# Seams between out product and FFN: residual stores and row scaling on GpSimd, more residual buffers, the last tile's squares and transposes placed

## The chip, the cores and the metric

The kernel runs on one core of a Trainium2 chip. The metric is the device time of one execution in microseconds (us); "before" was timed in 3 runs. Engines go by the names of the profile: PE is TensorE, PEld its weight load, DVE VectorE, ACT ScalarE, POOL GpSimd, SP the engine that issues most DMAs.

## The reference, cut to what matters

Two layers on 1024 tokens of width 1024. Layer 0 mixes with two groups of attention heads, layer 1 with a recurrent block. Each layer ends with a SwiGLU feed-forward network (FFN) of width 2816. Every sub-layer has a norm ahead of it and one behind it:

```
def rmsnorm(x, g):
    y = x * lax.rsqrt(jnp.mean(x * x, axis=-1, keepdims=True) + RMS_EPS)
    return y * g

for layer in range(2):
    h = rmsnorm(x, norm_mix_pre[layer])
    m = mixer(h)                       # ends with a product by w_out
    x = x + rmsnorm(m, norm_mix_post[layer])
    h = rmsnorm(x, norm_ffn_pre[layer])
    f = (silu(h @ w_gate) * (h @ w_up)) @ w_down
    x = x + rmsnorm(f, norm_ffn_post[layer])
```

## The kernel before, in words

Nearly every product is made in three passes: each operand is split into a high part (an ACT cast, L96, L525, L620, L736) and a low part (a DVE subtraction, L89, L526, L621, L737), and PE adds high by high, high by low and low by high. The FFN products go by Strassen's scheme: seven block products for gate and up (`strassen` in `gate_up`, L545 to L547 are its matmuls), and a like scheme in `down` (L625 to L627).

The program runs attention, `out_product`, `gate_up`, `down`, the recurrent block, `out_product`, `gate_up`, `down`. The text says seam A for the passage from the first `out_product` to the first `gate_up` (about 590 to 640 us), seam B for the second (about 1580 to 1620 us), and the two `down` stages are down(0) (its end at about 1250 us) and the last down (2140 us to the end).

`out_product` makes the mixer's product in eight tiles of 128 tokens: tiles 0 to 2 and 3 to 5 in three passes, tiles 6 and 7 as plain matmuls (L458). After each tile come two norms. `post_norm` loads the tile's old residual rows (`self.load`, L188, into one of the `nx` buffers), squares the product on ACT (L171; two halves, whose sums POOL adds, L173), makes 1/sqrt on POOL (L174, L175), multiplies by the gain on DVE (L219), adds the residual on DVE (L222) and stores the new residual by SP (L224). `pre_norm` squares that row again (L171), goes through POOL again, scales the row on ACT (L196), and PE turns it (eight transposes of 128x128, L204). `HiddenS.take` copies the turned halves out of PSUM (L85) and builds the right operands of the seven Strassen products, `hS`: high and low parts of the blocks themselves, and of four differences `tf` of them (L89 makes these differences on DVE, then L96 and L89 split them). `down` calls the same two norms for its own eight tiles of 128 rows; down(0) feeds the recurrent block through `HiddenT` (L57, L58), and the last down stores to the output and has no `pre_norm`.

`gate_up` makes the first gate block in two halves of tokens: the early half (tiles 0 to 3) and then the late half (tiles 4 to 7). So the early half's 84 matmuls can run while tiles 4 to 7 are still in their norms. Its weights, `raw`, are first multiplied by the norm's gain (L514, eight ACT instructions of 128x256 for one weight block).

What sets the order: each engine's queue is written by a scheduler of the framework when the kernel is built, from the dependencies, the buffers of each pool (`bufs`) and its own costs; `issue_after(x)` forbids it to place an instruction ahead of x. On the chip each engine takes its queue strictly in order.

Of the kernel before, what the change touches and what calls it, by code (L numbers as in the profile page):

```python
# [61 lines left out]
class HiddenS:  # L62
# [18 lines left out]
    def take(self, t, pst, scratch, pool):  # L81
# [7 lines left out]
        sub = lambda o, x, y: nc.vector.tensor_tensor(o, x, y, op=ALU.subtract)  # L89
        sub(tf[:, 0], b12, b11)  # L90
# [3 lines left out]
        cols = slice(64 * t, 64 * t + 64)  # L94
        for src, (h, l) in zip((hf[:, :, :, lo], hf[:, 1:2, :, hi], tf), self.g):
            self.last = nc.scalar.copy(h[:, :, :, cols], src).ins  # L96
            sub(l[:, :, :, cols], src, h[:, :, :, cols].bitcast(F32))


class Trunk:  # L100
# [64 lines left out]
    def rstd(self, pool, parts, junk):  # L165
# [4 lines left out]
        for p, o in zip(parts, ss):  # L170
            self.squared = nc.scalar.activation(junk, p, AF.Square, accum_out=o).ins  # L171
        if len(parts) == 2:
            nc.gpsimd.tensor_tensor(ss[0], ss[0], ss[1], op=ALU.add)  # L173
        nc.gpsimd.tensor_scalar(rs, ss[0], 1.0 / D, EPS, op0=ALU.mult, op1=ALU.add)  # L174
# [15 lines left out]
    def pre_norm(self, pool, x, h, g, sink, t, psum):  # L190
# [4 lines left out]
        if g is None:  # L195
            nc.scalar.activation(h, x, AF.Copy, scale=rs)  # L196
        else:
            self.scaled = nc.vector.scalar_tensor_tensor(h, x, rs, g, op0=ALU.mult, op1=ALU.mult).ins
        pst = []
        for q in range(2):  # L200
            ps = psum()
            for j in range(4):
                kt = 4 * q + j
                nc.tensor.transpose(ps[:, j * P:(j + 1) * P], h[:, kt * P:(kt + 1) * P], self.ident)  # L204
            pst.append(ps.rearrange("p (a b) -> p a b", a=4))
        sink.take(t, pst, h, pool)

    def post_norm(self, ms, mg, x_src, x_dst, t, gpost, sink, pool):
# [3 lines left out]
        x = pool.tile([P, D], F32, tag="nx", bufs=2, name=self.uid("x"))  # L212
# [5 lines left out]
        for c, m in ms:  # L218
            nc.vector.tensor_tensor(mg[:, c], m, gpost[:, c], op=ALU.mult)  # L219
        if mg is not ms[0][1]:  # L220
            rs = self.rstd(pool, [m for _, m in ms], junk)
        nc.vector.scalar_tensor_tensor(x, mg, rs, x, op0=ALU.mult, op1=ALU.add)  # L222
        for k, (d, s) in enumerate(rows(t, x_dst)):
            (nc.scalar if k and sink is None else nc.sync).dma_start(s, x[d, :])  # L224
        if sink is not None:
            self.pre_norm(pool, x, mg, None, sink, t, self.psum_t)
# [217 lines left out]
    def out_product(self, ap, aT, w, x_src, x_dst, gpost_v, sink, kts):  # L444
# [16 lines left out]
        def norm(t, ps):  # L461
            mg = ap.tile([P, D], F32, tag="mg", bufs=3, name=self.uid("mg"))
            ms = [(slice(i * 512, (i + 1) * 512), p) for i, p in enumerate(ps)]
            self.post_norm(ms, mg, x_src, x_dst, t, gpost, sink, ap)
# [517 lines left out]
```

## Time and profile before

| | |
|---|---|
| runs timed | 2254.22, 2256.64, 2258.45 us; median 2256.64 |
| the profiled execution | 2259.16 us, its span in the trace 2257.4 us |
| PE busy | 2209.1 us, 98% of the span |
| DVE busy | 1550.9 us, 69% |
| ACT busy | 1148.2 us, 51% |
| POOL busy | 166.8 us, 7% |

The profiled execution is 2.5 us above the median, and 1.76 us of it lie outside the span. A line such as L204 is a line of the kernel before, as printed above; the kernel after has other numbers. In a row of the timeline the first number is the start in us from the span's start, the second the duration, and the square brackets hold the idle time just before and what ended it.

### The profile page before, as it was taken

The page shows a single profiled execution, that of the slowest core. Times are in us where ns is not written, and L with a number is a line of the kernel's source. Part 1 is how long each engine was busy: PE and PEld are TensorE (multiplying, and loading weights), DVE is VectorE, ACT ScalarE, POOL GpSimd, SP SyncE. Part 2 cuts the span into 40 slices and gives each one's busy share as a digit, 9 for nine tenths or more (in the row PEclk, how much of TensorE's full clock was granted, in tenths as well). Part 3 has the DMA queues.
Part 4 walks back from the last instruction along what each step waited for, and adds up shares of the span by engine and source line. Part 5 has one row for each costly group of instructions (what it writes and reads, how often), then busy time and mean ns, then how long its engine had stood idle before and what let it go on. Part 6 is the DMA issues. An engine that isn't in the chain of part 4 may idle for free. (4 is left out here: it accounts for less than half of the span.)

```text
span 2257.4 us, 30651 instructions
## 1 busy us (share of the span) xinstructions
PE 2209.1 (98%) x11166; PEld 1810.3 (80%) x11166; DVE 1550.9 (69%) x2517; ACT 1148.2 (51%) x2132; POOL 166.8 (7%) x370
## 2 busy tenths in 40 slices
PE   8999999999999999999999999999999999999997
PEld 8888888877688888888887777887788888888875
DVE  5776765464677777776767787536777767669665
ACT  4545455464765444432436567527755454425433
POOL 2111212131100000000001100001100000000010
PEclk9999999999999999999999999999999999999998
DMA  5101011125623323235558511358233333237476
GB/s 169 45 29 34 24 43 46 54 98 151 222 88 111 119 89 122 89 131 184 173 163 256 135 52 47 90 185 270 76 117 107 112 99 118 93 112 267 130 203 189
DMA packets 187131, 273.12 MB, mean 121 GB/s; under 512 B 13922, under 2 KB 115298, under 8 KB 186979
## 3 DMA queue, kind: packets, MB, share of 16 engines
q1 hardware_dynamic: 186338, 269.06, 37.8%
q10 hardware_dynamic: 640, 2.10, 0.3%
q8 instruction: 88, 1.44, 0.3%
q14 instruction: 65, 0.52, 0.1%
HBM read 205.57 MB, written 65.54 MB: 120 GB/s over the span
## 5 line engine op out<-in xcount | busy, mean ns | idle before, releaser
L545 PE MATMUL ps<-hS,q 128*128 128x512 f32 (+1 forms) x1288 | 491.4, 383 | 2.8 <-ACT hS L96 2.8
L546 PE MATMUL ps<-hS,q 128*128 128x512 f32 (+1 forms) x1288 | 491.3, 382 | 0.0
L547 PE MATMUL ps<-hS,q 128*128 128x512 f32 (+1 forms) x1288 | 489.8, 382 | 0.0
L526 DVE TENSOR_TENSOR q<-raw,q 128x512 fp32r<-128x512 f32 x308 | 204.5, 686 | 176.9 <-ACT q L525 176.4
L545 PEld LDWEIGHTS ps<-hS,q 128*128 128x128 f32 x1288 | 244.1, 190 | 49.6 <-ACT hS L96 3.4
L546 PEld LDWEIGHTS ps<-hS,q 128*128 128x128 f32 x1288 | 244.3, 190 | 46.6 <-DVE hS L89 0.4
L547 PEld LDWEIGHTS ps<-hS,q 128*128 128x128 f32 x1288 | 244.4, 190 | 45.7
L525 ACT CAST q<-raw 128x512 fp32r<-128x512 f32 x308 | 177.4, 616 | 166.2 <-DVE raw L534 136.8
L626 PE MATMUL ps<-o,o 128*128 128x512 f32 x616 | 241.3, 392 | 2.8 <-DVE o L621 2.8
L627 PE MATMUL ps<-o,o 128*128 128x512 f32 x616 | 238.9, 392 | 0.5 <-DVE o L737 0.5
L625 PE MATMUL ps<-o,o 128*128 128x512 f32 x616 | 221.4, 393 | 10.3 <-ACT o L736 6.2
L514 ACT ACTIVATE raw<-raw,gcol 128x256 f32<-128x256 f32 x352 | 150.2, 498 | 149.9 <-DMA raw<-in_ffn_w_up_dram 73.0
L620 ACT CAST o<-raw 128x512 fp32r<-128x512 f32 x206 | 123.7, 620 | 197.6 <-PE ps L627 56.7
L621 DVE TENSOR_TENSOR o<-raw,o 128x512 fp32r<-128x512 f32 x206 | 137.8, 688 | 65.2 <-ACT o L620 64.5
L625 PEld LDWEIGHTS ps<-o,o 128*128 128x128 f32 x616 | 116.1, 189 | 38.4 <-ACT o L620 7.4
L626 PEld LDWEIGHTS ps<-o,o 128*128 128x128 f32 x616 | 116.5, 189 | 28.9 <-DVE o L621 4.7
L151 DVE TENSOR_TENSOR wlo<-raw,whi 128x1024 fp32r<-128x1024 f32 x76 | 92.8, 1222 | 65.7 <-ACT whi L150 63.5
L627 PEld LDWEIGHTS ps<-o,o 128*128 128x128 f32 x616 | 116.4, 189 | 24.8 <-DVE o L737 0.9
L174 POOL TENSOR_SCALAR rs<-ss 128x1 f32<-128x1 f32 x64 | 30.2, 472 | 1275.5 <-ACT junk L171 1171.2
L150 ACT CAST whi<-raw 128x1024 fp32r<-128x1024 f32 x76 | 79.8, 1052 | 59.2 <-PE ps L162 24.7
L365 ACT COPY pt<-tr 128x512 f32<-128x512 f32 (+1 forms) x128 | 65.5, 528 | 81.1 <-PE tr L361 80.5
L161 PE MATMUL psq<-hT,whi 128*128 128x512 f32 x256 | 101.2, 395 | 1.1 <-DVE v L260 1.1
(193 smaller groups left out, 4249.5 us busy)
## 6 DMA issues: line engine op xcount, KB each, us to landing
raw<-in_ffn_w_down_dram SPq DMA_DIRECT2D x96, 256.0 KB, 4.4
raw<-in_ffn_w_gate_dram SPq DMA_DIRECT2D x44, 512.0 KB, 4.3
raw<-in_ffn_w_up_dram SPq DMA_DIRECT2D x44, 512.0 KB, 4.4
gS<-c SPq DMA_DIRECT2D x88, 256.0 KB, 3.7
raw<-gS SPq DMA_DIRECT2D x88, 256.0 KB, 2.9
gA<-c SPq DMA_DIRECT2D x66, 256.0 KB, 3.3
raw<-in_attn_w_in_dram SPq DMA_DIRECT2D x24, 512.0 KB, 4.1
raw<-in_attn_w_out_dram SPq DMA_DIRECT2D x24, 512.0 KB, 4.5
```

The costliest lines, as they stand in the source:

```text
L161: nc.tensor.matmul(ps, wh[:, kt, cols], hh[:, kt, :], start=kt == 0, stop=False)
L514: nc.scalar.activation(raw[:, i], raw[:, i], AF.Copy, scale=gain[:, 4 * k + i:4 * k + i + 1])
L525: self.last = nc.scalar.copy(t[:, 0], src).ins
L526: nc.vector.tensor_tensor(t[:, 1], src, t[:, 0].bitcast(F32), op=ALU.subtract)
L545: nc.tensor.matmul(ps, a[:, 0, kt, :], bh, start=kt == 0, stop=False)
L546: nc.tensor.matmul(ps, a[:, 0, kt, :], bl, start=False, stop=False)
L547: nc.tensor.matmul(ps, a[:, 1, kt, :], bh, start=False, stop=kt == 3)
L620: nc.scalar.copy(t[:, 0], src)
L621: tt(t[:, 1], src, t[:, 0].bitcast(F32), op=ALU.subtract)
L625: nc.tensor.matmul(ps, a[0], b[:, 0], start=first, stop=False)
L626: nc.tensor.matmul(ps, a[0], b[:, 1], start=False, stop=False)
L627: nc.tensor.matmul(ps, a[1], b[:, 0], start=False, stop=last)
```

## The change

- `rstd` has the mean's factor in the square (`scale=D ** -0.5`) and adds EPS to the first half's sum, so after the last square POOL has two instructions where it had three for sums of two parts.
- `pre_norm` without a gain scales the row on GpSimd, as two instructions of 128x512, and the residual is stored from GpSimd's DMA queue, in the code behind the scaling. In the last down the stores of seven tiles go by GpSimd, those of the last tile by SP and ACT.
- The residual buffers `nx` go from two to three (tile 5 of `out_product` uses a further one), and in the last down there are four. To make room, `act` has two buffers instead of three.
- Tiles 6 and 7: both `post_norm` are written first, then both `pre_norm`; tile 6's `take` is issued after tile 7's squares and gain product (`last_m`).
- `gate_up`: the gain products of the first gate and up weights (16 instructions of 128x256 for each layer) move from ACT to GpSimd; the splits S3, S1 and S4 of the first gate block come after `last_m`; the last product of the early half (`A22`, 12 matmuls) comes after tile 7's last transpose (`turned`).
- `HiddenS.take` splits the plain blocks first, then makes the differences `tf` and splits them, and the single block last.

```diff
@@ HiddenS.take
+        def split(src, g):
+            h, l = (o[:, :, :, cols] for o in g)
+            self.last = nc.scalar.copy(h, src).ins
+            sub(l, src, h.bitcast(F32))
+
+        split(hf[:, :, :, lo], self.g[0])
         sub(tf[:, 0], b12, b11)
         sub(tf[:, 2], b22, b12)
         sub(tf[:, 1], b22, tf[:, 0])
         sub(tf[:, 3], tf[:, 1], b21)
-        cols = slice(64 * t, 64 * t + 64)
-        for src, (h, l) in zip((hf[:, :, :, lo], hf[:, 1:2, :, hi], tf), self.g):
-            self.last = nc.scalar.copy(h[:, :, :, cols], src).ins
-            sub(l[:, :, :, cols], src, h[:, :, :, cols].bitcast(F32))
+        split(tf, self.g[2])
+        split(hf[:, 1:2, :, hi], self.g[1])
@@ rstd
-        for p, o in zip(parts, ss):
-            self.squared = nc.scalar.activation(junk, p, AF.Square, accum_out=o).ins
-        if len(parts) == 2:
-            nc.gpsimd.tensor_tensor(ss[0], ss[0], ss[1], op=ALU.add)
-        nc.gpsimd.tensor_scalar(rs, ss[0], 1.0 / D, EPS, op0=ALU.mult, op1=ALU.add)
+        eps = EPS
+        for i, (p, o) in enumerate(zip(parts, ss)):
+            self.squared = nc.scalar.activation(junk, p, AF.Square, scale=D ** -0.5, accum_out=o).ins
+            if i < len(parts) - 1:
+                nc.gpsimd.tensor_scalar(o, o, eps, None, op0=ALU.add)
+                eps = o
+        nc.gpsimd.tensor_scalar(rs, ss[-1], eps, None, op0=ALU.add)
         nc.gpsimd.tensor_tensor(rs, rs, self.neghalf, op=ALU.pow)
@@ pre_norm
         if g is None:
-            nc.scalar.activation(h, x, AF.Copy, scale=rs)
+            for i in range(2):
+                cs = slice(i * 512, (i + 1) * 512)
+                nc.gpsimd.tensor_scalar(h[:, cs], x[:, cs], rs, 1.0, op0=ALU.mult, op1=ALU.mult)
+            then()
...
-        sink.take(t, pst, h, pool)
+        with self.behind(behind):
+            sink.take(t, pst, h, pool)
@@ post_norm
-        x = pool.tile([P, D], F32, tag="nx", bufs=2, name=self.uid("x"))
+        if x is None:
+            x = pool.tile([P, D], F32, tag="nx", bufs=3, name=self.uid("x"))
...
+        self.last_m = [self.squared, scaled]
         nc.vector.scalar_tensor_tensor(x, mg, rs, x, op0=ALU.mult, op1=ALU.add)
-        for k, (d, s) in enumerate(rows(t, x_dst)):
-            (nc.scalar if k and sink is None else nc.sync).dma_start(s, x[d, :])
-        if sink is not None:
-            self.pre_norm(pool, x, mg, None, sink, t, self.psum_t)
+        def store():
+            for k, (d, s) in enumerate(rows(t, x_dst)):
+                (stores or [nc.gpsimd] * 2)[k].dma_start(s, x[d, :])
+        if sink is None:
+            store()
+        if later is not None:
+            later.append(lambda b: self.pre_norm(pool, x, mg, None, sink, t, self.psum_t, b, store))
+        elif sink is not None:
+            self.pre_norm(pool, x, mg, None, sink, t, self.psum_t, then=store)
@@ out_product
+            x = self.apool.tile([P, 1152], F32, tag="first", name=self.uid("x"))[:, :D] if t == 5 else None
+            self.post_norm(ms, mg, x_src, x_dst, t, gpost, sink, ap, later, x)
...
-            norm(6 + t, ps)
+            norm(6 + t, ps, later)
+        for pre, b in zip(later, (self.last_m, ())):
+            pre(b)
@@ gate_up, load
-                        nc.scalar.activation(raw[:, i], raw[:, i], AF.Copy, scale=gain[:, 4 * k + i:4 * k + i + 1])
+                        g = gain[:, 4 * k + i:4 * k + i + 1]
+                        if j == 0:
+                            nc.gpsimd.tensor_scalar(raw[:, i], raw[:, i], g, 1.0, op0=ALU.mult, op1=ALU.mult)
+                        else:
+                            nc.scalar.activation(raw[:, i], raw[:, i], AF.Copy, scale=g)
...
-            split("S3", a21)
-            split("S1", a22)
-            tt(a12, a12, a11, op=ALU.subtract)
-            split("S4", a12)
+            with self.behind(behind):
+                split("S3", a21)
+                split("S1", a22)
+                tt(a12, a12, a11, op=ALU.subtract)
+                split("S4", a12)
@@ gate_up, strassen
-            tt(u3, u3, product(new(), q["A22"], 6, cols), op=ALU.subtract)
+            with self.behind(behind):
+                p4 = product(new(), q["A22"], 6, cols)
+            tt(u3, u3, p4, op=ALU.subtract)
@@ gate_up
-            qg = load(wg, j, ["w"] * 7, self.last if j == 1 else None)
+            qg = load(wg, j, ["w"] * 7, self.last if j == 1 else None, () if j else self.last_m)
...
-                strassen([first[:, i] for i in range(4)], qg, early)
+                strassen([first[:, i] for i in range(4)], qg, early, [self.turned])
@@ down
-            with make_sink() as sink:
+            with make_sink() as sink, self.pool("late", "right") as late:
+                if sink is not None:
+                    late = None
...
+                    stores = [nc.sync, nc.scalar] if sink is None and (r, a) == (0, 3) else None
+                    x = late.tile([P, D], F32, tag="nx", bufs=4, name=self.uid("x")) if late else None
+                    self.post_norm(ms, mg, x_src, x_dst, (r, a), gpost, sink, ap, None, x, stores)
```

Three places show what this does to the order. The first is seam A, where PE passes from the early half of the first gate block to the late half; `ps_6761` (before) and `ps_6767` (after) hold the early half's last product, `mg_6522` and `mg_6496` tile 7's scaled row, `ps_6779` the late half's first product. PE before:

```order
L545 MATMUL ps_6761<-hS_5640,q_6656 128x256
L546 MATMUL ps_6761<-hS_5641,q_6656 128x256
L547 MATMUL ps_6761<-hS_5640,q_6656 128x256
L204 MATMUL pst_6544<-ident,mg_6522 128x128 x4
L204 MATMUL pst_6549<-ident,mg_6522 128x128 x4
L545 MATMUL ps_6779<-hS_5636,q_6650 128x256
```

PE after, at the same place, where twelve matmuls on `ps_6767` in all follow the transposes before the late half starts:

```order
L597 MATMUL ps_6753<-hS_5638,q_6661 128x256
L224 MATMUL pst_6550<-ident,mg_6496 128x128 x4
L224 MATMUL pst_6555<-ident,mg_6496 128x128 x4
L595 MATMUL ps_6767<-hS_5640,q_6662 128x256
L596 MATMUL ps_6767<-hS_5641,q_6662 128x256
L597 MATMUL ps_6767<-hS_5640,q_6662 128x256
```

Tile 7's transposes have moved ahead of the early half's last product. DVE at the same place, before, where `mg_6459` is tile 6's row, `tf_6493` and `tf_6556` are the differences of tiles 6 and 7, and `hS_5641` is the low part of the differences:

```order
L89 TENSOR_TENSOR hS_5641<-tf_6398,hS_5640 128x16x64
L571 TENSOR_TENSOR first_6675<-first_6675,ps_6761 128x256
L89 TENSOR_TENSOR tf_6493<-mg_6459 128x256 x2
L89 TENSOR_TENSOR tf_6493<-mg_6459,tf_6493 128x256
L89 TENSOR_TENSOR tf_6493<-tf_6493,mg_6459 128x256
L89 TENSOR_TENSOR hS_5637<-mg_6522,hS_5636 128x8x64
L89 TENSOR_TENSOR hS_5639<-mg_6522,hS_5638 128x4x64
L89 TENSOR_TENSOR hS_5641<-tf_6493,hS_5640 128x16x64
L89 TENSOR_TENSOR tf_6556<-mg_6522 128x256 x2
```

DVE after (`mg_6463` and `tf_6531` are tile 6's, `mg_6496` and `tf_6562` tile 7's):

```order
L89 TENSOR_TENSOR tf_6531<-mg_6463 128x256 x2
L624 TENSOR_TENSOR first_6681<-first_6681,ps_6767 128x256
L89 TENSOR_TENSOR hS_5637<-mg_6496,hS_5636 128x8x64
L89 TENSOR_TENSOR hS_5639<-mg_6496,hS_5638 128x4x64
L89 TENSOR_TENSOR tf_6531<-mg_6463,tf_6531 128x256
L89 TENSOR_TENSOR tf_6531<-tf_6531,mg_6463 128x256
L89 TENSOR_TENSOR hS_5641<-tf_6531,hS_5640 128x16x64
L575 TENSOR_TENSOR q_6904<-raw_6892,q_6904 128x512
L89 TENSOR_TENSOR tf_6562<-mg_6496 128x256 x2
```

The second half of tile 6's differences now stands behind tile 7's plain blocks. The second place is POOL in seam A for tiles 6 and 7. Before:

```order
L173 TENSOR_TENSOR ss_6466<-ss_6466,ss_6467 128x1
L174 TENSOR_SCALAR rs_6465<-ss_6466 128x1
L175 TENSOR_TENSOR rs_6465<-rs_6465,neghalf 128x1
L174 TENSOR_SCALAR rs_6475<-ss_6476 128x1
L175 TENSOR_TENSOR rs_6475<-rs_6475,neghalf 128x1
L173 TENSOR_TENSOR ss_6529<-ss_6529,ss_6530 128x1
L174 TENSOR_SCALAR rs_6528<-ss_6529 128x1
L175 TENSOR_TENSOR rs_6528<-rs_6528,neghalf 128x1
```

POOL after (`x_6464` and `x_6497` are the residual rows of tiles 6 and 7):

```order
L252 DMA xs_89<-x_6464 128x1024
L181 TENSOR_SCALAR ss_6503<-ss_6503 128x1
L183 TENSOR_SCALAR rs_6502<-ss_6504,ss_6503 128x1
L184 TENSOR_TENSOR rs_6502<-rs_6502,neghalf 128x1
L183 TENSOR_SCALAR rs_6511<-ss_6512 128x1
L184 TENSOR_TENSOR rs_6511<-rs_6511,neghalf 128x1
L215 TENSOR_SCALAR mg_6463<-x_6464,rs_6511 128x512 x2
L252 DMA xs_89<-x_6497 128x1024
L183 TENSOR_SCALAR rs_6542<-ss_6543 128x1
L184 TENSOR_TENSOR rs_6542<-rs_6542,neghalf 128x1
L215 TENSOR_SCALAR mg_6496<-x_6497,rs_6542 128x512 x2
L561 TENSOR_SCALAR raw_6898<-raw_6898,gcol 128x256 x4
```

Stores and scaling have entered the queue; the store of tile 7's residual stands ahead of tile 7's second 1/sqrt. The third place is SP in the last down, where the weights and left operands of the product `p3` are loaded (`raw`) and residual rows (`x`) move. Before:

```order
L718 DMA raw_19412<-in_ffn_w_down_dram 128x512
L224 DMA out_dram<-x_19230 64x1024
L188 DMA x_19256<-xs_91 64x1024
L224 DMA out_dram<-x_19243 64x1024
L188 DMA x_19256<-xs_91 64x1024
L717 DMA raw_19433<-gS_1_7_14574 128x512
```

SP after:

```order
L776 DMA raw_19439<-in_ffn_w_down_dram 128x512
L197 DMA x_19649<-xs_91 64x1024
L775 DMA raw_19460<-gS_1_7_14598 128x512
L776 DMA raw_19460<-in_ffn_w_down_dram 128x512
L775 DMA raw_19481<-gS_1_8_14599 128x512
L776 DMA raw_19481<-in_ffn_w_down_dram 128x512
```

The stores have left SP's queue, and of the loads one half row is left ahead of the `raw` with number 7: `x_19649` belongs to the fifth tile and takes a buffer that the first tile's store has to leave.

More of the change, by code (lines that the diff above doesn't have):

```diff
@@ L489, in out_product @@
             rows.append(raw)
-            acts.append(act(kt, 6, 2, ap, 3, ("act", "ah", "al")[i % 3]))
+            acts.append(act(kt, 6, 2, ap, (3, 3, 2)[i % 3], ("ah", "al", "act")[i % 3]))
+        later = []
         for t in range(2):
```

35 lines of the change are left out of this document (23 added, 12 removed).

## Prediction, made before the changed kernel had run

> **What bounds the kernel now.** I read the page first (busy shares and the granted clock), then PE's waits by line and longest case, then the timeline of each place where a long wait stands.
>
> ```profile
> PE 2209.1 (98%) x11166; PEld 1810.3 (80%) x11166; DVE 1550.9 (69%) x2517; ACT 1148.2 (51%) x2132; POOL 166.8 (7%) x370
> ```
>
> ```profile
> PE ps L625 <- ACT o L736: 6.2, 3, 3.5
> PE pst L204 <- ACT mg L196: 5.7, 2, 2.9
> PE ps L625 <- ACT o L620: 4.0, 4, 1.7
> ...
> PE ps L626 <- DVE o L621: 2.8, 4, 2.1
> PE ps L545 <- ACT hS L96: 2.8, 2, 1.4
> ```
>
> PE is the bound nearly everywhere; it has 48.3 us of idle time in all (2257.4 less 2209.1). The columns of the second fence are us in total, cases and the longest. Two of its lines belong to the seams: 5.7 us for the scaled row before tile 7's transposes and 2.8 us for the high parts behind them, two cases each, so about 4.25 us for each seam. The other three belong to the two `down` stages. But a wait costs more than its own length, as a table of stretches of seam A shows (columns: stretch, its length, busy PE, PEld, DVE, ACT, POOL, granted clock, DMA share, GB/s):
>
> ```profile
> 600.00:612.00 12.00, 12.00 (x35) 5.77 (x34) 9.61 (x16) 8.33 (x15) 1.78 (x4) 1.00 0.16 51
> 612.00:627.00 15.00, 12.76 (x102) 11.94 (x100) 14.79 (x31) 13.30 (x28) 3.52 (x7) 0.99 0.42 137
> 627.00:631.00 4.00, 1.99 (x9) 1.59 (x9) 2.70 (x7) 2.50 (x5) 0.00 (x0) 0.50 0.01 2
> 631.00:637.00 6.00, 6.00 (x27) 5.78 (x27) 4.59 (x8) 3.12 (x6) 0.00 (x0) 0.50 0.00 0
> ```
>
> From 612 to 627 DVE is full and ACT nearly; then PE starves, and the granted clock is 0.50 until 637. Two matmuls of 256 columns stand 0.12 us apart at full clock and 0.21 us apart at 0.50:
>
> ```profile
> 624.36 0.28 PE L546 MATMUL ps<-hS,q 128*128 128x256 f32 x1
> 624.48 0.28 PE L547 MATMUL ps<-hS,q 128*128 128x256 f32 x1
> 627.69 1.97 PE L204 MATMUL pst<-ident,mg 128*128 128x128 f32 x8 [2.93 <-ACT mg L196]
> 630.98 0.80 PE L545 MATMUL ps<-hS,q 128*128 128x256 f32 x2 [1.32 <-ACT hS L96]
> ...
> 632.30 0.41 PE L545 MATMUL ps<-hS,q 128*128 128x256 f32 x1
> 632.52 0.41 PE L546 MATMUL ps<-hS,q 128*128 128x256 f32 x1
> ...
> 636.57 0.85 PE L545 MATMUL ps<-hS,q 128*128 128x256 f32 x4
> ```
>
> So each us at half clock loses 0.44 us of matmul work (1 less 0.12/0.213). The Trainium skill ("TensorE: Matmul & The Clock Gate", part 1) describes a gate that looks at PE's activity in windows of a few us; the 0.50 of these rows agrees with its half clock, and nothing below is taken from it.
>
> **Seam A, term by term.** Tile 7's last plain matmul ends at about 612.7, yet its way to the transposes is long:
>
> ```profile
> 618.43 0.60 ACT L171 ACTIVATE junk<-ps 128x512 bf16<-128x512 f32 x1
> ...
> 620.59 0.22 ACT L171 ACTIVATION_READ_ACCUMULATOR junk<-ps 128x1 f32 x1
> ...
> 624.20 1.06 ACT L171 ACTIVATE mg<-x 128x1024 f32<-128x1024 f32 x1 [1.47 <-DVE x L222]
> ...
> 626.49 1.15 ACT L196 ACTIVATE mg<-x,rs 128x1024 f32<-128x1024 f32 x1 [0.20 <-POOL rs L175]
> ...
> 635.07 1.05 ACT L96 CAST hS<-tf 128x1024 fp32r<-128x1024 f32 x1 [2.88 <-DVE tf L89]
> ```
>
> The first square waits 5.7 us in ACT's queue, behind tile 6's scaling, casts and copies. From their end (620.81) to the transposes (627.69) it takes 6.9 us. In the new order they stand ahead of tile 6's second square, so they can end at 615.5: 612.7, two squares of 0.8, and 1.2 us for ACT work in front. Behind them the chain is the same but for POOL's part:
>
> ```profile
> L343 POOL TENSOR_SCALAR pr<-pr,sm 128x512 f32<-128x512 f32 x8 | 5.5, 695 | 7.1 <-DVE sm L342 7.1
> L343 POOL TENSOR_SCALAR pr<-pr,sm 128x256 f32<-128x256 f32 x8 | 3.8, 482 | 6.5 <-DVE sm L342 5.3 <-PE sc L329 0.9
> ```
>
> A scaling of 128x512 by a column takes 0.70 us on POOL (attention has the same instruction), so a row costs 1.39 us where ACT took 1.15: 0.24 more. One POOL instruction less saves 0.28. The store now in front of the second 1/sqrt is issued by POOL, which no row of before shows; the nearest is SP's issue, 0.34 us, and the far end I set at 1.45 us, the longest a POOL instruction took beside a busy DVE:
>
> ```profile
> 624.20 0.34 SPq L224 DMA_DIRECT2D xs<-x  x1
> ```
>
> ```profile
> 2178.68 0.19 POOL L174 TENSOR_SCALAR rs<-ss 128x1 f32<-128x1 f32 x1 [571.38 <-ACT junk L171]
> 2178.95 1.45 POOL L175 TENSOR_TENSOR rs<-rs,neghalf 128x1 f32<-128x1 f32 x1
> ```
>
> I take 0.34 for the store since POOL writes no tile for it, and add 1.0 us because tile 6's 1/sqrt and scaling stand in POOL's queue ahead of tile 7's second part. Transposes ready: 615.5 + 6.9 + 0.24 - 0.28 + 0.34 + 1.0 = 623.7, against 627.69; ends of the unknown costs 622.7 and 626. PE arrives there at 624.6 less the twelve matmuls moved behind (12 x 0.12 = 1.44), so 623.2: a wait of 0.5 us instead of 2.93. At full clock eight transposes take 1.0 us, so they end at 624.7 instead of 629.66.
>
> What is late next are the differences `tf`, made and split on DVE:
>
> ```profile
> 613.88 0.69 DVE L526 TENSOR_TENSOR q<-raw,q 128x512 fp32r<-128x512 f32 x1
> 614.48 0.42 DVE L89 TENSOR_TENSOR tf<-tf,mg 128x256 f32<-128x256 f32 x1
> ```
>
>  Before, the high part was ready at 636.12, 6.5 us after the transposes, and the late half's third product began at 636.57; the slow clock hid that wait. In the new order, between tile 7's transposes and its `tf`, DVE also has two differences of tile 6 (0.42 each) and a split of the up weights (0.69); 1.5 us more, 8.0 in all, so 632.7. PE covers from 624.7 only the twelve moved matmuls (1.44), a short wait of about 0.6 for the plain blocks, and 24 matmuls of the late half (2.88): until 629.6. There a new wait of 3.1 us appears, ended by ACT's cast of `tf`. The third product begins at 632.7 instead of 636.57: 3.9 us won; bounds 1.5 (transposes at 626) and 5.4 (no extra DVE work in the way). A wait like this one brought a half clock of 3.4 us or more in some cases (2.93 us here did) and none in another (2.11 us at 2187.65, below), so I charge half of 3.4 x 0.44 = 1.5 us. Seam A: 3.9 - 0.75 = about 3.1 us won.
>
> **The cover of what moves off ACT and SP.** The 16 gain products of a layer (0.48 us each on POOL) cost PE nothing as long as POOL is through with the early ones before tile 3; POOL works 1.78 of 12 us there before. The stores leave SP, where nothing waited for them in seam A. Three residual buffers end this idle time of DVE, which was not PE's:
>
> ```profile
> 596.65 1.28 DVE L222 SCALAR_TENSOR_TENSOR x<-mg,rs,x 128x1024 f32<-128x1024 f32 x1 [5.51 <-DMA x<-in_x_dram]
> ```
>
> Its worth is that DVE enters the full stretch with less in arrears; without it I would not trust the 1.2 us above.
>
> **Seam B** has the same order:
>
> ```profile
> 1615.14 1.04 ACT L96 CAST hS<-tf 128x1024 fp32r<-128x1024 f32 x1 [2.88 <-DVE tf L89]
> ```
>
> ```profile
> 1608.53 1.09 PE L204 MATMUL pst<-ident,mg 128*128 128x128 f32 x8 [2.77 <-ACT mg L196]
> ```
>
> PE comes to the transposes at 1608.53 - 2.77 - 1.44 = 1604.3 and by the same 0.5 us of wait and 1.0 of work ends them at 1605.8; plus 8.0 is 1613.8 against 1616.2 for the cast's end before: 2.4 won, less 0.75: 1.6 us.
>
> **The down stages.** In the last down these are the long waits of PE, and SP's queue around the first:
>
> ```profile
> 2187.65 0.50 PE L626 MATMUL ps<-o,o 128*128 128x512 f32 x1 [2.11 <-DVE o L621]
> 2196.93 1.19 PE L625 MATMUL ps<-o,o 128*128 128x512 f32 x4 [1.69 <-ACT o L620]
> ...
> 2217.48 0.79 PE L625 MATMUL ps<-o,o 128*128 128x512 f32 x1 [3.51 <-ACT o L736]
> ```
>
> ```profile
> 2184.09 0.51 SPq L224 DMA_DIRECT2D out_dram<-x  x1
> 2187.91 0.45 SPq L188 DMA_DIRECT2D x<-xs  x1
> ...
> 2189.77 0.72 SPq L717 DMA_DIRECT2D raw<-gS  x1
> ```
>
> The wait of 1.69 us is for the `raw` issued at 2189.77, which stood behind a residual load that waited 3.3 us for a store to land. Four buffers take three of four such loads away. The fifth tile's half load still stands ahead of that same `raw`, now behind a store from POOL's queue, so I count that wait as it is (bounds 1.7 won, 1.5 lost). The wait of 2.11 us is DVE's: in the new order more of the norms' work stands ahead of that split, up to two of DVE's 1.28 us steps, so 0 to 1.5 lost; the smaller waits behind may win 1. Sum zero, -3 to +3. The 3.51 us wait is for a load in a stretch that the DMA engines fill; it stays. In down(0) a wait of 2.01 us (cast L736, at 1247.5) ends with a load whose buffer DVE frees; no store stands in front, so I count 0.5 won from ACT's and SP's lighter queues, -2 to +1.5. At the end of the program POOL's chain loses one instruction:
>
> ```profile
> 2249.90 0.19 POOL L173 TENSOR_TENSOR ss<-ss,ss 128x1 f32<-128x1 f32 x1 [3.56 <-ACT junk L171]
> 2250.18 0.19 POOL L174 TENSOR_SCALAR rs<-ss 128x1 f32<-128x1 f32 x1
> ```
>
> That is 0.28 us, all of it on the path.
>
> Sum: 3.1 + 1.6 + 0.5 + 0 + 0.3 = 5.5 us won, so 2253.7 for the profiled execution's 2259.16. That execution stands 2.5 above the median; against the median of 2256.64 the forecast is 2251.
>
> **The rivals.**
>
> Slower: POOL and DVE shut each other out in the seams. The pair at 2178.68 and 2178.95 speaks for it: 0.19 us alone, 1.45 where 0.55 is usual, while DVE ran. POOL's six instructions on tile 7's way (two for 1/sqrt twice, two for the scaling) would each take 0.9 us more (1.45 less 0.55), 5.4 in all: transposes ready at 629.1 instead of 627.69, ended at 630.1, the third product at 638.1 by the same 8.0, 1.5 us later than before; with 1.2 for the half clock that goes on behind it, 2.7 lost at each seam. With one us lost in the last down: 2256.64 + 2 x 2.7 + 1 = 2263. DVE, busy for 31.7 of the 37 us from 600 to 637, has little room to wait for POOL in turn. It turns to a loss once the mean stretch passes about 0.65 us, where its six times eat the 3.9 won. Against it: in the seam before, L174 and L175 ran at 0.38 and 0.55 us beside tile 7. The Trainium skill ("SBUF — State Buffer", section "SBUF: two separate sides") says that a DVE instruction with two SBUF inputs and a GpSimd instruction reading SBUF hold one port pair as an exclusive lock, so that the later one waits for the whole of the other. By that rule the shut-out would be complete and the seams would win nothing; DVE's instructions at the seam mostly have two SBUF inputs, but the short stretches of the row at hand do not bear a full shut-out out. It also says ("DMA: Bandwidth & Descriptors", section "SWDGE vs HWDGE vs iDMA") that GpSimd writes a DMA's descriptors itself, which SP's and ACT's queues don't need; no row of before shows a price.
>
> Full recovery: the new wait for `tf` is short, the half clock does not come, and the stores' leaving SP ends the 1.69 us. Each seam then wins its 4.25 us of waits and the 0.44 of its half clock, 4.25 + 0.44 x 6 = 6.9 us in seam A (10 us at half clock less the 4 idle in it), I take 5.5 for B, where the half clock is shorter, and the down stages 2: about 2242. Against it: DVE's list behind the transposes has not become shorter.
>
> Nothing to measure: the transposes come early, but the late half stands as long for `tf`, and the half clock comes with that wait. Each seam wins 1 us or less: 2255.
>
> **How the numbers follow.** Forecast (1.5 to 9 us won) 0.42; full recovery 0.15; nothing to measure 0.20; slower 0.23. The range leaves out the outer half of the second and the last: 2242 to 2262. The forecast's own range is 2247.5 to 2255. About 0.2%, 4.5 us, can be told from no change. Three quarters of the forecast's chance and all of the full recovery lie under 2252.1: 0.47 faster; the rest of the forecast, the third rival and a little of the slower case make 0.31; slower 0.22.
>
> **What would show it.** Right: in seam A tile 7's squares before 616, its transposes before 625, a new wait of PE ahead of the late half's third product ended by the cast of `tf`, and a granted clock of 0.50 for under 7 us. Wrong: POOL scalings well over 0.70 us each with DVE busy beside them; PE waits at tile 6's transposes, which now stand behind tile 7's squares; PE waits in the last down that grow by more than 2 us because the `raw` with number 7 comes late.

## The result, and the profile after

The changed kernel takes 2294.64 us (median of 4 runs, 2291.13 to 2294.91), the kernel before 2256.03 in the runs beside it: 1.68% slower, ratio 1.0168 with a 95% interval of 1.0156 to 1.018. The forecast was 2251, the range ended at 2262. The span of the profiled execution is 2292.8 us. First the page's busy shares, then PE's waits by line (total us, cases, longest), of the kernel after; L595 is a gate or up matmul, L678 and L679 are matmuls of `down`, L224 the transposes.

```profile
PE 2219.0 (97%) x11166; PEld 1815.2 (79%) x11166; DVE 1559.3 (68%) x2517; ACT 1113.9 (49%) x2076; POOL 280.4 (12%) x496
```

```profile
PE ps L678 <- ACT o L673: 11.8, 6, 6.3
PE ps L595 <- ACT hS L94: 7.5, 2, 3.7
PE pst L224 <- DVE hT L58: 7.3, 4, 6.3
PE pst L224 <- POOL mg L215: 4.4, 2, 2.2
PE ps L679 <- DVE o L674: 4.3, 4, 3.3
...
PE ps L595 <- ACT q L574: 2.8, 2, 1.5
PE ps L678 <- ACT o L794: 2.6, 2, 1.5
```

POOL works 114 us more, ACT 34 less, and most long waits of PE have grown or are new; the one for the cast that was L736 (6.2 us) and is now L794 (2.6 us) has shrunk. To see where the time went I summed, stage by stage, what PE lost: the distance from each matmul's start to the next beyond the median distance for that shape (so waits and half clock count alike). The stages are taken wide, 560 to 680 us for seam A, 1200 to 1300 for down(0) and the start of the recurrent block, 1540 to 1700 for seam B, and from 2140 on for the last down. Us lost by stage in one profiled execution of each kernel, with the median of the runs behind it:

| kernel | seam A | down(0) and the start of the recurrent block | seam B | last down | time |
|---|---|---|---|---|---|
| before | 21.5 | 10.2 | 20.1 | 13.3 | 2256.0 |
| after | 27.1 | 22.6 | 27.8 | 24.2 | 2294.6 |

The four stages make 36.6 us more lost, which is all of the 35.4 us by which the two profiled spans differ (the medians differ by 38.6). In seam A, PE's waits after:

```profile
618.80 0.39 PE L595 MATMUL ps<-hS,q 128*128 128x256 f32 x1 [1.27 <-ACT q L574]
...
622.03 1.12 PE L224 MATMUL pst<-ident,mg 128*128 128x128 f32 x4 [2.21 <-POOL mg L215]
...
629.30 1.04 PE L224 MATMUL pst<-ident,mg 128*128 128x128 f32 x8
...
639.73 0.74 PE L595 MATMUL ps<-hS,q 128*128 128x256 f32 x4 [3.73 <-ACT hS L94]
```

PE waits for the split S3, then for tile 6's row (the row at 622.03); tile 7's transposes, at 629.30, come without a wait. Seam B has the same waits (1.54 us for S3, 2.21 for tile 6's row, 3.73 for `tf`). The last row is the late half's third product, at 639.73 where it was 636.57, behind the wait for `tf`. POOL's rows behind tile 6's and tile 7's second squares:

```profile
618.39 1.31 POOL L183 TENSOR_SCALAR rs<-ss 128x1 f32<-128x1 f32 x1
619.79 0.86 POOL L184 TENSOR_TENSOR rs<-rs,neghalf 128x1 f32<-128x1 f32 x1
620.74 2.33 POOL L215 TENSOR_SCALAR mg<-x,rs 128x512 f32<-128x512 f32 x2
...
624.77 1.36 POOL L215 TENSOR_SCALAR mg<-x,rs 128x512 f32<-128x512 f32 x2
```

Tile 6's row costs 2.33 us, tile 7's 1.36. The granted clock in the stretches that were shown of before (columns as there):

```profile
612.00:627.00 15.00, 11.51 (x72) 10.70 (x71) 11.64 (x20) 10.33 (x21) 9.47 (x14) 0.79 0.32 95
627.00:631.00 4.00, 4.00 (x33) 4.00 (x33) 2.70 (x5) 2.18 (x5) 1.11 (x3) 0.93 0.10 40
631.00:637.00 6.00, 4.15 (x31) 3.54 (x29) 4.85 (x11) 2.56 (x5) 0.00 (x0) 1.00 0.00 0
637.00:645.00 8.00, 5.27 (x31) 5.27 (x32) 5.20 (x10) 4.67 (x8) 0.00 (x0) 0.79 0.01 2
```

The half clock has come twice, behind the wait for tile 6 and behind the wait for `tf`, instead of once. By the clock column it lasted about 6.9 us (0.21 of 15 us and 0.07 of 4, doubled) and about 3.4 us (0.21 of 8, doubled). That is about 10 us together, as in the one long stretch of before: what has grown is the waiting.

At the start of the recurrent block the longest wait is for transposes of a row that POOL scales behind a store and a 1/sqrt (PE first, then POOL):

```profile
1284.30 1.09 PE L224 MATMUL pst<-ident,m 128*128 128x128 f32 x4 [6.27 <-DVE hT L58]
```

```profile
1278.55 1.16 POOL L252 DMA_DIRECT2D xs<-x  x2 [1.62 <-DVE x L248]
1279.79 0.98 POOL L183 TENSOR_SCALAR rs<-ss 128x1 f32<-128x1 f32 x1
1280.85 1.40 POOL L184 TENSOR_TENSOR rs<-rs,neghalf 128x1 f32<-128x1 f32 x1
1282.35 2.43 POOL L215 TENSOR_SCALAR m<-x,rs 128x512 f32<-128x512 f32 x2
```

The profile names DVE's take of the tile ahead as the releaser (its first half ended at 1284.15); POOL's two instructions took 1.76 and 0.69 us, so the first scaled half was there at 1284.11. Both are late, so neither alone explains the 6.27 us.

In the last down, SP, ACT, POOL and PE:

```profile
2206.28 0.43 SPq L776 DMA_DIRECT2D raw<-in_ffn_w_down_dram  x1
2224.98 0.45 SPq L197 DMA_DIRECT2D x<-xs  x1
2225.54 1.37 SPq L775 DMA_DIRECT2D raw<-gS  x1
```

```profile
2231.20 0.62 ACT L673 CAST o<-raw 128x512 fp32r<-128x512 f32 x1 [17.05 <-DMA raw<-gS]
```

```profile
2211.93 3.73 POOL L184 TENSOR_TENSOR rs<-rs,neghalf 128x1 f32<-128x1 f32 x1
...
2219.76 4.29 POOL L252 DMA_DIRECT2D out_dram<-x  x8
```

```profile
2233.11 2.07 PE L678 MATMUL ps<-o,o 128*128 128x512 f32 x4 [6.33 <-ACT o L673]
```

SP stands from 2206.7 to 2224.98 at the half load of the fifth tile. The buffer it wants is left by the first tile's store, which stands in POOL's queue behind all four tiles' 1/sqrt (one of them 3.73 us long) and is issued at 2219.76. The operands of `p3` stand behind that load, ACT idles for 17 us, and PE runs dry.

### The profile page after: what moved, and what is told of

The parts are those of the page before. It is cut to its first block, busy times and chain, and to the rows that moved or that the text cites. A ratio compares the mean times of both kernels' runs of the same rounds, so it can differ in the third digit from the quotient of the medians.

```text
span 2292.8 us, 30778 instructions
## 1 busy us (share of the span) xinstructions
PE 2219.0 (97%) x11166; PEld 1815.2 (79%) x11166; DVE 1559.3 (68%) x2517; ACT 1113.9 (49%) x2076; POOL 280.4 (12%) x496
## 5 line engine op out<-in xcount | busy, mean ns | idle before, releaser
L595 PE MATMUL ps<-hS,q 128*128 128x512 f32 (+1 forms) x1288 | 492.8, 384 | 10.3 <-ACT hS L94 7.5
L595 PEld LDWEIGHTS ps<-hS,q 128*128 128x128 f32 x1288 | 244.3, 190 | 58.1 <-ACT hS L94 8.3
L679 PE MATMUL ps<-o,o 128*128 128x512 f32 x616 | 243.8, 396 | 4.3 <-DVE o L674 4.3
L678 PE MATMUL ps<-o,o 128*128 128x512 f32 x616 | 223.3, 398 | 14.9 <-ACT o L673 11.8
L563 ACT ACTIVATE raw<-raw,gcol 128x256 f32<-128x256 f32 x320 | 137.0, 498 | 123.9 <-DMA raw<-in_ffn_w_up_dram 72.1
L678 PEld LDWEIGHTS ps<-o,o 128*128 128x128 f32 x616 | 117.7, 192 | 44.0 <-ACT o L673 15.5
L679 PEld LDWEIGHTS ps<-o,o 128*128 128x128 f32 x616 | 117.4, 191 | 30.6 <-DVE o L674 6.2
L156 ACT CAST whi<-raw 128x1024 fp32r<-128x1024 f32 x76 | 79.8, 1052 | 63.3 <-PE ps L168 23.8
```

What stands on the lines that cost most here:

```text
L563: nc.scalar.activation(raw[:, i], raw[:, i], AF.Copy, scale=g)
L595: nc.tensor.matmul(ps, a[:, 0, kt, :], bh, start=kt == 0, stop=False)
L678: nc.tensor.matmul(ps, a[0], b[:, 0], start=first, stop=False)
L679: nc.tensor.matmul(ps, a[0], b[:, 1], start=False, stop=False)
```

## The experiments

The first four each alter one part of the changed kernel. Times are medians; the kernel before is 2254.6 to 2255.6 beside all of them, and ratios are to it. A difference of about 1 us between two runs of this section therefore says nothing.

**late8**: eight residual buffers in the last down, so no load waits for a store.

```diff
-x = late.tile([P, D], F32, tag="nx", bufs=4, ...)
+x = late.tile([P, D], F32, tag="nx", bufs=8, ...)
```

> The changed kernel with eight residual buffers in the last down instead of four; nothing else. Theory: in the last down SP's queue stood from 2206.7 to 2225.0 at one half load that waited for a buffer, that is for a store in POOL's queue, and the operands of p3 stood behind it (ACT idle 17.05 us, PE 6.33 us). With eight buffers no load waits for a store: PE's 6.33 us wait goes, 8 to 12 us faster than the changed kernel, 2283 to 2287 us. Rival: DVE and POOL holding each other up (pow at 3.73 us) make the loss of the last down; then the time stays within 3 us of 2294.6.

Measured: 2282.1 us (1.0115, 1.0099 to 1.0131), 12.5 less than the changed kernel. PE's loss in the last down falls from 24.2 to 8.2 us, those of the three other stages stay within 0.4. (The profiled execution took 2277.2 us, 4.9 less than the median, so the stages show more than the medians' 12.5.) The half load in front of the operands was the cause. What a 1/sqrt step of 3.73 us would cost without that load is not shown: in this kernel the longest one there is 1.46 us.

**scale_act**: the row scaling back on ACT.

```diff
-for i in range(2):
-    cs = slice(i * 512, (i + 1) * 512)
-    nc.gpsimd.tensor_scalar(h[:, cs], x[:, cs], rs, 1.0, op0=ALU.mult, op1=ALU.mult)
+nc.scalar.activation(h, x, AF.Copy, scale=rs)
```

> The changed kernel with the row scaling back on ACT (one instruction of 128x1024); nothing else. Theory: the scaled rows come late because POOL takes 2.3 to 3.2 us for a row beside DVE, and PE waits for them (2.2 us at each seam with the half clock behind it, 6.3 us at 1284): 12 to 20 us faster than the changed kernel, 2275 to 2283 us. Rival: the placement of tile 7's squares ahead of tile 6's makes the loss at the seams, and the order of the queues that of the recurrent block's start: less than 6 us faster.

Measured: 2277.6 us (1.0098, 1.0083 to 1.0113), 17.0 less. The gain is spread: 4.3 and 3.2 us at the seams, 4.5 in down(0), 6.0 in the last down. No row is scaled there, but the queues were written anew, and PE's wait behind the half load is 4.20 us instead of 6.33: POOL issues the first tile's store 8.5 us after it began the first 1/sqrt (2193.41 to 2201.90), where it was 12.6 us in the changed kernel (2207.19 to 2219.76).

**place_off**: tiles 6 and 7 without placement.

```diff
-norm(6 + t, ps, later)
+norm(6 + t, ps)
-qg = load(wg, j, ["w"] * 7, ..., () if j else self.last_m)
+qg = load(wg, j, ["w"] * 7, ...)
-strassen(..., qg, early, [self.turned])
+strassen(..., qg, early)
```

> The changed kernel without the placement at the seams: each of tiles 6 and 7 has its pre_norm right behind its post_norm, and the splits S3, S1, S4 and the early half's last product are tied to nothing. Theory: the placement costs tile 6 its place on ACT and PE waits 1.3 us for a split and 2.2 us for tile 6's row at each seam; without it the seams are 3 to 6 us faster each, 2283 to 2289 us. Rival: POOL's scaling alone makes the seams slow; then no gain or a loss, 2292 to 2300 us, since tile 7 comes later again.

Measured: 2285.4 us (1.0131, 1.0113 to 1.0148), 9.3 less. But the seams lose 26.2 and 27.8 us, hardly less than with the placement: the waits for the split, for tile 6 and for `tf` go, and one of 4.9 us for tile 7's row on POOL comes instead. The time was won in other stages, most in the last down (24.2 to 19.4), where POOL again issues the first store sooner (9.6 us after the first 1/sqrt began). Why the queues came out so is not shown. The time fell in the expected band for another reason.

**stores_hw**: the stores back on SP, in the last down on SP and ACT.

```diff
-(stores or [nc.gpsimd] * 2)[k].dma_start(s, x[d, :])
+(nc.scalar if k and sink is None else nc.sync).dma_start(s, x[d, :])
```

> The changed kernel with the residual stores back on SP (in the last down SP and ACT, as before); nothing else. Theory: frees the last down of the wait behind POOL's stores, and takes about 0.6 us of store issue from POOL in front of each second 1/sqrt: 8 to 15 us faster, 2280 to 2287 us. Rival: SP's loads stand behind the stores again as before, and the four buffers don't help: within 4 us of 2294.6.

Measured: 2285.8 us (1.0131, 1.0116 to 1.0146), 8.8 less; the last down falls to 12.9 us lost, the other stages stay within 1.6. The next four take parts off together, with eight buffers; their edits are those of the runs above.

**scale_late8**: scaling on ACT and eight buffers.

> The changed kernel with the row scaling on ACT and eight residual buffers in the last down. Theory: the two causes lie in different stages (scaling: seams and the start of the recurrent block; buffers: last down), so their gains of 12.5 and 17.0 us add, less about 6 us that the scaling run already had in the last down: 2267 to 2273 us. Rival: they share a cause (POOL's queue), and the sum is clearly smaller: 2274 us or more.

Measured: 2267.9 us (1.0064, 1.0049 to 1.0079), in the expected band.

**scale_place_late8**: that, without the placement.

> As the kernel with scaling on ACT and eight buffers, and without the placement of tiles 6 and 7 at the seams. Theory that the placement is bad in itself: each seam loses the 4 to 5 us wait for tile 7's row that the scaling run still shows, 4 to 9 us faster than that kernel, 2260 to 2266 us. Rival: the placement is good once ACT scales, and without it tile 7 comes later: same or up to 6 us slower.

Measured: 2267.2 us (1.0057, 1.004 to 1.0073). The same; neither the 4 us gain nor a loss. In this kernel the placement neither helps nor harms.

**scale_stores_late8**: scaling on ACT, eight buffers, stores on SP and ACT.

> As the kernel with scaling on ACT and eight buffers, with the stores back on SP and ACT. Theory: POOL is left with 1/sqrt and the gains; the stores cost POOL 0.63 us each ahead of a 1/sqrt, and mostly in down(0) and the seams: 2 to 5 us faster than that kernel, 2264 to 2268 us. Rival: SP's loads stand behind the stores again; then 3 to 8 us slower, 2272 to 2278 us.

Measured: 2257.1 us (1.0014, 1.0004 to 1.0023), 10.8 less than with POOL's stores, more than either theory said. Down(0) falls from 18.0 to 11.8 us lost.

**only_bufs8**: scaling, stores, gains, placement and take as before; the buffers, the shorter POOL chain and eight buffers are left.

Beside the edits of scale_act, stores_hw, place_off and late8 this one has:

```diff
-if j == 0:
-    nc.gpsimd.tensor_scalar(raw[:, i], raw[:, i], g, 1.0, op0=ALU.mult, op1=ALU.mult)
-else:
-    nc.scalar.activation(raw[:, i], raw[:, i], AF.Copy, scale=g)
+nc.scalar.activation(raw[:, i], raw[:, i], AF.Copy, scale=g)
...
-split(hf[:, :, :, lo], self.g[0])
 sub(tf[:, 0], b12, b11)
...
-split(tf, self.g[2])
+split(hf[:, :, :, lo], self.g[0])
 split(hf[:, 1:2, :, hi], self.g[1])
+split(tf, self.g[2])
```

> The kernel before with the buffers of the change (three residual buffers, two of act, one common first tile), its shorter POOL chain and eight residual buffers in the last down; scaling, stores, gains, placement and take order as before. Theory: what remains is a gain, 5 us in the last down (its PE losses go from 13.3 to 8.2 us with eight buffers) and 0.3 at the end: 2249 to 2252 us, faster than before. Rival: two act buffers or the new order of the scheduler cost as much elsewhere: 2255 to 2262 us.

Measured: 2250.3 us (0.9984, 0.9975 to 0.9994): faster than before. This is the base to which the next runs add one part each, by leaving out the edit that undoes it. Us lost by stage, and times:

| added to only_bufs8 | seam A | down(0), recurrent start | seam B | last down | time | above the base |
|---|---|---|---|---|---|---|
| nothing | 18.2 | 11.4 | 18.1 | 9.2 | 2250.3 | |
| row scaling on POOL | 23.8 | 21.6 | 24.1 | 7.6 | 2274.3 | 24.1 |
| half a row on POOL | 22.0 | 13.5 | 22.0 | 12.0 | 2262.2 | 12.0 |
| gains on POOL | 23.2 | 11.1 | 23.7 | 10.3 | 2264.6 | 14.4 |
| new order of the take | 23.1 | 12.3 | 24.9 | 8.3 | 2261.2 | 11.0 |
| stores on POOL | 18.3 | 20.2 | 18.8 | 8.6 | 2257.0 | 6.7 |
| placement | 18.6 | 10.8 | 18.4 | 9.7 | 2250.6 | 0.4 |
| placement and take | 22.4 | 10.5 | 22.4 | 10.8 | 2259.0 | 8.7 |

**alone_scale**

> The kernel with only the buffers of the change, and the row scaling on GpSimd in addition. Theory: a scaled row takes 1.4 us on POOL where DVE is idle and 2.3 to 3.2 us where it is busy, against 1.15 on ACT; tile 7's row comes about 2 us later, and the next tiles wait behind it: 8 to 14 us slower than 2250.3, 2258 to 2264 us. Rival: ACT is what delays the rows, and taking the scaling off it pays for it: within 3 us of the base.

Measured: 2274.3 us, far above the band. Each seam loses 6 us more, and down(0) 10. The trace shows the price of a row (two instructions) where DVE is idle, and twice beside DVE:

```profile
591.07 1.37 POOL L215 TENSOR_SCALAR mg<-x,rs 128x512 f32<-128x512 f32 x2
...
603.07 2.37 POOL L215 TENSOR_SCALAR mg<-x,rs 128x512 f32<-128x512 f32 x2
...
613.72 2.58 POOL L215 TENSOR_SCALAR mg<-x,rs 128x512 f32<-128x512 f32 x2
```

**half_scale**: half of each row on POOL, half on ACT.

```diff
+nc.gpsimd.tensor_scalar(h[:, 512:], x[:, 512:], rs, 1.0, op0=ALU.mult, op1=ALU.mult)
+nc.scalar.activation(h[:, :512], x[:, :512], AF.Copy, scale=rs)
```

> As the kernel with only the buffers and the scaling on GpSimd (2274.3 us), but half a row on GpSimd and the other half on ACT. Theory that POOL's time for a row beside DVE (2.1 to 2.6 us) makes the loss: a half takes 1.0 to 1.3 us there, no longer than ACT's whole row, so most of the 24 us go: 2252 to 2260 us. Rival that the place of the scaling in POOL's queue (the 1/sqrt of other tiles behind it) makes it: more than half stays, 2263 to 2272 us.

Measured: 2262.2 us, between the two bands: half the work costs half the time in all, but not stage by stage. At the seams 3.8 and 3.9 of the 5.6 and 6.0 us stay, in down(0) 2.1 of 10.2, and the last down, where nothing is scaled, loses 2.8 more than the base. So in down(0) POOL's time for a row decides; at the seams it does not alone.

**alone_gains**

> The kernel with only the buffers of the change, and the first gain products on GpSimd in addition. Theory: they are done ahead of tile 3 or behind tile 7 and free 8 us of ACT in each seam's surroundings: within 2 us of 2250.3, 2248 to 2252 us. Rival: they stand in POOL's queue ahead of a tile's 1/sqrt, or hold up DVE: 2253 us or more.

Measured: 2264.6 us; the rival. In this kernel's seam A four gain products stand ahead of tile 7's first 1/sqrt; POOL waits 2.18 us for the load of their weights, and they take 3.7 us beside DVE. PE waits 4.09 us for tile 7's row:

```profile
617.75 3.71 POOL L559 TENSOR_SCALAR raw<-raw,gcol 128x256 f32<-128x256 f32 x4 [2.18 <-DMA raw<-in_ffn_w_up_dram]
621.44 0.28 POOL L183 TENSOR_SCALAR rs<-ss,ss 128x1 f32<-128x1 f32 x1
```

```profile
628.08 1.60 PE L222 MATMUL pst<-ident,mg 128*128 128x128 f32 x8 [4.09 <-ACT mg L213]
```

In the changed kernel those four come behind tile 7's scaling. The runs also show the gains beside the placement and the new take: scale_stores_late8 (2257.1 us, 1.0014) is place_take (below, 2259.0 us, 1.0013) with the gains on POOL, and by their ratios to before the two can't be told apart. There the wait of about 4 us at seam A is one for tile 7's row with the gains and one for `tf` without them.

**alone_take**

> The kernel with only the buffers of the change and the new order of the take in addition. Theory: tile 7's plain blocks come earlier and its differences later: the 1.4 us wait behind the transposes goes and a wait at the late half's third product comes, 2249 to 2253 us. Rival: the plain blocks first is a pure gain: 2246 to 2248 us.

Measured: 2261.2 us, above both bands. The wait for `tf` at the late half's third product is there, as long as in the changed kernel:

```profile
635.97 1.23 PE L593 MATMUL ps<-hS,q 128*128 128x256 f32 x4 [3.73 <-ACT hS L94]
```

**alone_stores**

> The kernel with only the buffers of the change (three residual buffers, eight in the last down), and the residual stores on GpSimd's queue in addition; scaling, gains, placement and take order as before. Base without the stores: 2250.3 us. Theory: a store takes POOL 0.6 us for a tile of 512 KB and 1.15 us for two halves, and it waits in POOL's queue for the residual row, so that any 1/sqrt behind it waits too; 7 to 12 us slower, 2257 to 2262 us, more than half of it in down(0). Rival: stores on POOL cost only beside the other POOL work; alone within 3 us of the base.

Measured: 2257.0 us, at the lower edge of the band. All of the loss is in down(0), where more than half was expected: there the second 1/sqrt of a tile begins behind a store of 1.15 us (two halves), and PE waits 5.02 us for the first operands of the recurrent block.

```profile
1260.20 1.15 POOL L250 DMA_DIRECT2D xs<-x  x2 [1.80 <-DVE x L246]
1261.64 0.55 POOL L183 TENSOR_SCALAR rs<-ss 128x1 f32<-128x1 f32 x1 [0.29 <-ACT m L179]
```

```profile
1273.85 0.80 PE L168 MATMUL ps<-hT,whi 128*128 128x512 f32 x1 [5.02 <-DVE hT L58]
```

**alone_place**

> The kernel with only the buffers of the change, and the placement of tiles 6 and 7 in addition. Base: at each seam PE waits 1.1 us for tile 7's row. Theory: the placement holds the splits S3, S1, S4 behind tile 7's squares and tile 6's second square behind them; PE then waits in the early half for splits and for tile 6, and behind tile 7 as long as before: 3 to 8 us slower, 2253 to 2258 us. Rival: with ACT free of nothing else it does what it is written for, the two waits of 1.1 us go: 2246 to 2249 us.

Measured: 2250.6 us, the base's time. The waits of 1.1 us for tile 7's row go as the rival said, and at each seam one of 0.6 us for a split and one of 1.54 us for `tf` come in their place.

**place_take**

> The kernel with only the buffers of the change, and the placement of tiles 6 and 7 and the new order of the take in addition; scaling, gains and stores as before. Theory: the placement alone moved the wait from tile 7's row to the differences (1.5 us at each seam), and the new order of the take makes these earlier: 2246 to 2250 us. Rival: the order of the take puts tile 7's plain parts ahead of tile 6's differences on DVE and the wait grows as in the changed kernel (3.7 us): 2252 to 2256 us.

Measured: 2259.0 us (1.0013, 1.0005 to 1.0022). The wait for `tf` is 4.1 us at each seam: the new take takes away what the placement gives.

**before_late8**: the kernel before with a pool of eight residual buffers in the last down.

```diff
+with self.pool("late", "right") as late:
...
+    x = late.tile([P, D], F32, tag="nx", bufs=8, ...)
-    self.post_norm(..., gpost, sink, ap)
+    self.post_norm(..., gpost, sink, ap, x)
```

> The kernel before with eight residual buffers in the last down; nothing else. Theory: the gain of the kernel with only the buffers comes mostly from the last down, where PE's losses went from 13.3 to 9.2 us: 3 to 5 us faster than before, 2250 to 2252 us. Rival: it comes from the seams (three buffers instead of two there, losses from 41.6 to 36.3 us): within 2 us of before.

Measured: 2250.3 us (0.9981, 0.9972 to 0.9991). That edit alone gains as much as the base of the table, and beats both kernels; the loss in the last down goes from 13.3 to 9.0 us. Neither this, the base nor the placement on it can be told from one another.

## Why the prediction was wrong, point by point

The sum had 3.1 us won in seam A, 1.6 in seam B, 0.5 in down(0), nothing in the last down. The two profiled executions give 5.6, 7.7, 12.4 and 10.9 us lost. The steps that failed are the path of tile 6, POOL's price of a row, the term of down(0), which had no POOL chain in it, and the bound of the blocked load in the last down.

- **Bound and seams.** That a wait of PE at the seams costs more than its own length, by the half clock behind it, was right, and so was the new wait for `tf`, ended by ACT's cast; it was put at 3.1 us and is 3.73.
- **Tile 7's squares** were to end at 615.5. The first begins at 615.45; the step put 1.2 us of ACT work ahead of them, and it was the gain product on DVE (ended at about 615.4) that ACT waited for.
- **Tile 6 was not in the sum.** The step "they stand ahead of tile 6's second square" counted what tile 7 gains and not what tile 6 loses: its square begins at 617.09 instead of 611.05, and PE comes to its transposes 2.2 us early. The last paragraph named this wait as a sign of error, with no price. It decides when PE reaches tile 7: the sum had PE there at 623.2 and waiting for a row ready at 623.7; POOL ended that row at 626.13, and PE came only at 629.30. The 1.27 us for S3, the 2.21 for tile 6 and about 2.4 for the matmuls at half clock between 622.03 and 627.6 (5.6 us at 0.44, an estimate) are nearly all of those 6.1 us. It was not the placement by itself: without it (place_off) the seams lose as much, by a wait of 4.9 us for tile 7's row, and alone it costs nothing (0.4 us).
- **POOL's price of a row**, 1.39 us from attention's 0.70, was the lower end taken as the value. It holds where DVE is idle; beside DVE it was 2.33 us for tile 6 here, and 2.09 to 2.58 us for the last three rows of seam A in alone_scale. Added alone, the scaling costs 24.1 us, more than any other part. Two rows of before had shown the stretch in the same seam: the prediction looked at tile 7's 1/sqrt (0.38 and 0.55 us), not at tile 6's, whose two steps took 0.52 and 1.00 us beside DVE:

```profile
608.10 0.52 POOL L174 TENSOR_SCALAR rs<-ss 128x1 f32<-128x1 f32 x1
608.70 1.00 POOL L175 TENSOR_TENSOR rs<-rs,neghalf 128x1 f32<-128x1 f32 x1
```

- **The take's order**: "1.5 us more" of DVE work in front of `tf` was right in kind. It measured 9.4 us from tile 7's transposes' end to the third product instead of 8.0, and alone costs 11.0 us; the sum set this against a gain of the transposes that did not come.
- **Gains "cost PE nothing"**: 14.4 us alone, where four of them came ahead of tile 7's 1/sqrt; POOL's idle share was looked at, not its queue. Beside the placement and the take they cost nothing that can be told, so this step may have held in the changed kernel; with the scaling on POOL it was not tried.
- **Stores**: in seam A free (18.2 and 18.3), where the sum charged 0.34 us for a store that took 0.63; in down(0), where the sum counted 0.5 won, 8.8 us lost. The down(0) term did not contain POOL's chain at all.
- **The last down**: the load in front of the operands was seen and bounded at 1.5 us lost. The last down lost 10.9 us more than before, and with eight buffers the kernel is 12.5 us faster. The bound took a store's landing and left out that the store is issued only behind the four tiles' 1/sqrt.
- **The slower rival** had the right mechanism and 2263, but put it in the wrong place: it stretched POOL on tile 7's way, 0.9 us an instruction. In seam A tile 7's six instructions took 0.28 to 0.69 us, about as long as where DVE is idle; the stretched ones were tile 6's ahead of them (1.31, 0.86 and 2.33 us). Down(0) was outside it, and the last down had 1 us.

Added one by one, scaling, gains, take, stores and placement cost 56.6 us; together (late8 less the base) 31.8. At the two seams alone the first three add 11.6, 10.6 and 11.7 us lost and all five 18.4 (26.7 and 28.0 against 18.2 and 18.1): the costs end in the same waits. In down(0) scaling and stores add 10.2 and 8.8, and 11.0 together. So a part's price depends on what stands beside it. Taken away one after the other, from late8 (2282.1 us) down to the base, they come to: scaling 14.2 (scale_late8), stores 10.8 (scale_stores_late8), gains nothing that can be told (place_take), take 8.3 (alone_place), placement 0.4. Other orders were tried only in part.

## What to carry to other kernels

Work moved to an engine that is idle 93% of the time is priced by what stands behind it in that engine's queue and by how busy its neighbour (here DVE) is at the place where it will run, not by its mean elsewhere. When a store moves to another queue, find the load that needs its buffer and what stands behind that load; more buffers, so that no load waits, are the safe form. Here that one number, put into the kernel before, gave 2250.3 us, and no kernel here was clearly faster. When an instruction is put ahead, price the one it passes.

## What the runs showed of the hardware

In the changed kernel a POOL scaling of 128x512 took 0.69 to 0.70 us with DVE idle and 0.68 to 2.58 beside it, and 1/sqrt's second step 0.54 to 0.57 and 0.54 to 3.73. DVE paid far less in turn: its differences `tf` of 128x256, with scaling on POOL (alone_scale) and without (only_bufs8), as total and as mean in ns:

```profile
L89 DVE TENSOR_TENSOR tf<-mg 128x256 f32<-128x256 f32 x32 | 13.8, 451 | 7.6 <-ACT mg L85 7.2
```

```profile
L89 DVE TENSOR_TENSOR tf<-mg 128x256 f32<-128x256 f32 x32 | 12.7, 422 | 7.3 <-ACT mg L85 6.7
```

The exclusive lock that the Trainium skill states ("SBUF — State Buffer", "SBUF: two separate sides") agrees in kind with the longest case, the 3.73 us from 2211.93 in the last down: DVE issued three instructions back to back, to 2215.23, and POOL's step ended at 2215.65.

```profile
2211.68 1.27 DVE L248 SCALAR_TENSOR_TENSOR x<-m,rs,x 128x1024 f32<-128x1024 f32 x1
2212.88 2.35 DVE L244 TENSOR_TENSOR m<-m,g 128x1024 f32<-128x1024 f32 x2
```

But there POOL got no turn between DVE's instructions, which the even-handed rule (who starts first holds the pair) does not lead one to expect. A store from POOL's queue held POOL for 0.63 us (512 KB, one DMA, seam A of the changed kernel) or 1.15 us (two halves); on SP's queue before the first of these took 0.34.
